# A one-column copy that holds GpSimd's weight remainders back near LayerNorm, two remainders on VectorE, and a new order of the state-space steps

## The chip, the cores and the metric

The kernel runs on one core of a Trainium2 chip. Its time is the device time of one execution in microseconds (us). The engines are named as the profile names them: PE is TensorE's matmul, PEld its weight load, DVE is VectorE, ACT is ScalarE, POOL is GpSimd, SP is SyncE, whose queue issues nearly all loads. L233 is line 233 of the kernel before.

## The reference

One sequence of 512 positions with 1024 channels goes through two residual layers, in float32. Each layer has a token mixer and then a SwiGLU channel mixer of hidden size 2816, and behind each of these four stands a LayerNorm with a residual:

```python
def reference(x, ...):
    h = x
    for i in range(DEPTH):                      # DEPTH = 2
        if i % 2 == 0:
            mix = s5_mixer(h, ...)              # state-space scan over positions, GELU, GLU, out-projection
        else:
            mix = stick_breaking_mixer(h, ...)  # 16 heads x 64, strictly causal, no softmax
        h = layer_norm(DEEPNORM_ALPHA * h + mix, ...)
        h = layer_norm(DEEPNORM_ALPHA * h + swiglu_ffn(h, ...), ...)
    return h
```

## The kernel before

**Split operands.** All large products run on PE in float32r, three matmuls for one (`mm3`, L350 to L352; `tm`, L369 to L371): an operand w is split in a high part (`wh`, a copy on ACT that rounds) and a remainder (`wl` = w - wh). The `Weights` object streams the weight chunks of 128 x 1024 through a ring of 37 buffers of 128 x 1024 (`Ring`, first in, first out). `load` issues the DMA on SP's queue (L226, L223 for pairs), `pump` splits chunk after chunk (L283 on ACT, L286 for the remainder). The remainder is formed on DVE unless `l_eng` names POOL. Activations are split in the same way (`xh`, `xl`; L345 on ACT, L346 on DVE).

**Feed-forward weights in pairs.** From the third row of blocks on (i = 2 to 21) the gate and up weights of a block are combined in seven operands (`split_pair`, through the helper `tt` at L233) for a product with fewer multiplications (`pair`). POOL does three operations of it: half of `s` (128 x 512), the remainder `gl` (128 x 1024) and half of `bl` (128 x 512). DVE does the rest. The x side needs sums and differences of halves of x, formed once per layer by `x_forms` on DVE (L422, then L346 into the tiles `xf`).

**The stages in order.** `ssm` (state space, PE order written out in `SSM_ORDER`), `ssm_end` (GLU and out-projection), `ffn(0)`, `attention`, `att_end` (its out-projection), `ffn(1)`. Where two stages meet, `tail` runs: for each of four tiles of 128 positions the last product steps of the projection, then LayerNorm `ln` on DVE (L390 residual, L392 and L394 statistics, L400 subtract and scale, L80 to L90 the inverse root, L403 the last step), then `tr`, which transposes the tile on PE (L415) and splits it. While the last tile is in LayerNorm, PE already starts the next stage on the first half of the positions (`nxt[0](lo)`, `nxt[1](lo)`). `tail` has `forms=True` behind the two mixers (called by `proj`), False behind the feed-forwards.

**Who remainders go to in `tail`.** From tile t = 1 on, `l_eng` is POOL, until `tail` ends. Inside the product steps of `proj`, `ws.pump(chunks[-1] + 2 * t)` at t = 1 and t = 2 splits the first feed-forward chunks ahead of their use. Behind attention (`begun=7`) only the last of eight chunks is left for t = 0 and 1, so that only t = 2 pumps, four chunks at once; behind the state space one chunk at t = 1 and two at t = 2 are left to pump. When the second half of the positions starts (`run` in `ffn_first`), the first weight pair (chunk i = 2) is split; the pair i = 3 is begun inside `pair(2)`.

**What sets the order.** Inside `tc.manual_schedule(engines=...)` the named engines run in program order: PE, DVE, ACT, POOL and SP in `ssm`; PE and DVE in `pair`. Elsewhere a planner orders each engine's queue by priority and readiness; `high_priority` puts LayerNorm ahead of other DVE work. In `SSM_ORDER` each word is a step with a block number: t, T transpose g on PE (L822), m, M multiply with x (L833), d9 nine filler matmuls (L840), k the kernel matrix (L867) whose result goes through DRAM (L876 out, L889 back in, step n), r and s the scan on DVE, y the output (L957), u a GLU part, p a weight chunk with its remainder on POOL, q one with its remainder on DVE, e a table on POOL.

Of the kernel before, what the change touches and what calls it, by code (L numbers as in the profile page):

```python
# [9 lines left out]
F32 = mybir.dt.float32  # L10
# [7 lines left out]
S = 512  # L18
D = 1024
KD = D // 128  # L20
# [25 lines left out]
def glu_items(text):  # L46
# [12 lines left out]


SSM_ORDER = (
# [3 lines left out]
)  # L65

# [93 lines left out]
class Ring:  # L160


    def __init__(self, pool, n):
        self.pool, self.free, self.n = pool, list(range(n)), 0
        self.slot = {}

    def get(self, name, dtype=F32R):
        i = self.free.pop(0)
        self.n += 1
        t = self.pool.tile([128, 1024], dtype, tag=f"s{i}", bufs=1, name=f"{name}_{self.n}")  # L170
        self.slot[t.name] = i
        return t
# [25 lines left out]
class Weights:  # L198


    def __init__(self, nc, ring):
        self.nc, self.ring = nc, ring
        self.src, self.raw, self.hl = [], {}, {}
        self.loaded = self.split = 0
        self.nraw = 3
        self.hold = True
        self.h_eng = self.l_eng = None

    def add(self, ap):
        self.src.append(ap)  # L210
# [19 lines left out]
    def split_pair(self, i, g, u):  # L230

        nc, V, G_, get = self.nc, self.nc.vector, self.nc.gpsimd, self.ring.get
        tt = lambda o, a, b, op=SUB, e=V: e.tensor_tensor(out=o, in0=a, in1=b, op=op)  # L233
        f = lambda t: t.bitcast(F32)
        lo, hi = slice(0, 512), slice(512, 1024)
        s1, s2 = self.sums
        gh, gl, bh, bl, c, sh, sl = tiles = [get("wf") for _ in range(7)]

        a = [(gh[:, lo], gl[:, lo]), (gh[:, hi], gl[:, hi]), (sh[:, hi], sl[:, hi]), (bh[:, lo], bl[:, lo]),
             (bh[:, hi], bl[:, hi]), (c[:, lo], c[:, hi]), (sh[:, lo], sl[:, lo])]  # L240
        self.hl[i] = dict(tiles=tiles, a=a)
        s = get("ws", F32)
        tt(s[:, lo], g[:, lo], u[:, lo], SUB, G_)
        nc.scalar.activation(gh, g, AF.Copy)  # L244
        nc.scalar.activation(bh[:, lo], u[:, hi], AF.Copy)
        tt(gl, g, f(gh), SUB, G_)
        tt(bl[:, lo], u[:, hi], f(bh[:, lo]), SUB, G_)
        yield
        tt(s1, u[:, lo], u[:, hi], ADD)
        tt(s2, s1, g[:, lo])  # L250
        tt(s[:, hi], g[:, hi], s2)
        nc.scalar.activation(bh[:, hi], s1, AF.Copy)
        nc.scalar.activation(c[:, lo], s2, AF.Copy)
        nc.scalar.activation(sh, s, AF.Copy)
        tt(bl[:, hi], s1, f(bh[:, hi]))
        tt(c[:, hi], s2, f(c[:, lo]))
        yield
        tt(sl, s, f(sh))
        self.ring.put(g, u, s)
        self.split += 1  # L260
        self.load(i + 1)

    def begin(self, i):

# [5 lines left out]
    def pump(self, upto):  # L270
        nc = self.nc
        upto = min(upto, len(self.src) - 1)
        while self.split <= upto:
            i = self.split
            self.load(i if isinstance(self.src[i], tuple) else i + self.nraw - 1)
            w = self.raw.pop(i)
            if isinstance(w, list):
                for _ in self.split_pair(i, *w):
                    pass
                continue  # L280
            h, l = self.ring.get("wh"), self.ring.get("wl")
            if self.h_eng is None:
                nc.scalar.activation(h, w, AF.Copy)  # L283
            else:
                self.h_eng.tensor_copy(h, w)
            (self.l_eng or nc.vector).tensor_tensor(out=l, in0=w, in1=h.bitcast(F32), op=SUB)  # L286
            self.ring.put(w)
            self.load(i + self.nraw)
            self.hl[i] = (h, l)
            self.split += 1  # L290
# [10 lines left out]
class Trunk:  # L301
# [195 lines left out]
    def tail(self, tiles, nxt, out=None, lag=1, fine=False, forms=False):  # L497


        def store(t):  # L500
            if out is None:
                with self.tc.high_priority(offset=1):
                    self.tr(t)
        todo = 0
        for t in range(4):
            steps = tiles[t]
            if t == 1:
                self.ws.l_eng = self.nc.gpsimd
            at = [max(0, len(steps) - 3)] if t >= lag and (t < 3 or not nxt) else []
            if t == 3 and lag > 1:  # L510
                at = [len(steps) // 4, len(steps) // 2]
            for i, f in enumerate(steps):
                if i in at and todo < t:
                    store(todo)
                    todo += 1
                f()
            with self.tc.high_priority(offset=800):
                self.ln(t, self.COLS[t == 3 and fine], None if out is None else out[t])
        self.ring.put(self.lng, self.lnb)
        if nxt:  # L520
            lo, hi = slice(0, S // 2), slice(S // 2, S)
            nxt[0](lo)
            if todo == 2:
                store(2)
            nxt[1](lo)
            if forms:
                E = mybir.EngineType
                f, g = self.x_forms(2), self.x_forms(3)
                next(f)
                next(g)  # L530
                with self.tc.manual_schedule(engines={E.Activation, E.DVE}):
                    next(f)
                    self.tr(3)
                    next(g)
                    for h in (f, g):
                        for _ in h:
                            pass
            else:
                store(3)
            nxt[0](hi)  # L540
            nxt[1](hi)
        else:
            store(3)
        self.ws.l_eng = None

    def ffn(self, l, nxt, out=None):
        nc, ws, ring = self.nc, self.ws, self.ring
# [13 lines left out]
        def ahead():  # L561

            ws.hold = True
            ws.pump(self.c_dn[l][0])
            yield
            take(1)
            yield
            ws.pump(self.c_dn[l][1])
            yield

        for i in range(KF):
            if i > 1:
                c = self.c_gu[l][i]
                if i == 2:
                    self.cv = ring.get("cv", F32)
                E = mybir.EngineType
                with self.tc.manual_schedule(engines={E.PE, E.DVE} | ({E.Activation} if i == KF - 1 else set())):
                    a = ws.get(c, 0)["a"]
                    self.pair(i, a, ws.begin(c + 1) if i < KF - 1 else ahead())
                ws.done(c)  # L580
            else:
                b = 2 * i
                s = self.tmp.tile([128, S], F32, tag="s", name="s")
                nc.scalar.activation(s, self.ps[:, b], AF.Silu)
                nc.vector.tensor_tensor(out=self.hidden(i), in0=s, in1=self.ps[:, b + 1], op=MUL)  # L585
# [500 lines left out]
    def proj(self, chunks, yt, nxt, order=None, begun=0):  # L1086

        ws, ring = self.ws, self.ring
        order = order or list(range(KD))
        tiles = []  # L1090
        for t in range(4):
            steps = []
            todo = [(m, c, n) for m, c in enumerate(self.COLS[t == 3]) for n in range(KD)]
            if t == 0:
                todo.sort(key=lambda a: a[2])
            for m, c, n in todo:
                    k = order[n]
                    if t < 2 and n < begun:
                        continue
                    def f(t=t, n=n, k=k, m=m, c=c):  # L1100
                        hl = ws.get(chunks[k], 0)
                        self.tm(t, hl, yt[k][:, 0:S], yt[k][:, S:], n == 0, n == KD - 1, (c,))
                        if t == 3 and m == 2:
                            ws.done(chunks[k])
                            ring.put(yt[k])
                        if m == 1 and n == 3 and t > 0 and t < 3:
                            ws.pump(chunks[-1] + 2 * t)
                    steps.append(f)
            tiles.append(steps)
        self.tail(tiles, nxt, lag=2 if begun else 1, fine=True, forms=True)  # L1110
# [317 lines left out]
```

## Time and profile before

| | |
|---|---|
| median of 3 runs | 1215.75 us (1214.12 to 1216.79) |
| profiled execution, its own time | 1223.04 us |
| its span, first to last instruction | 1221.3 us |
| mean granted TensorE clock | 0.991 |
| busy: PE, DVE, ACT, POOL | 1164.6, 897.0, 512.1, 383.4 us |
| POOL remainders of pairs (L233) | 80, 161.2 us busy |
| POOL remainders of chunks (L286) | 20, 49.5 us busy |

The profiled execution is one run with the profiler on, and a few microseconds longer than the plain runs. The page gives for each engine the time in which it worked. The list of waits gives, for an engine and line, who ended the wait, the total, how often, and the longest. A timeline row has start, duration, engine, line, operation, output and inputs, shapes, count, and in brackets the idle time of the engine just before with the one who ended it. A windows row has the stretch and the busy time in it of each engine, with the count of instructions that began.

### The profile page before, as it was taken

What the parts mean: (1) busy time and instruction counts of PE and PEld (TensorE: products, weight loads), DVE (VectorE), ACT (ScalarE), POOL (GpSimd) and SP (SyncE); (2) the same over time, 40 slices, a digit from 0 to 9 for tenths busy, and PEclk for the clock granted to TensorE, in tenths of its full rate; (3) what the DMA queues carried; (4) which work ended last, traced back from release to release, by engine and by line L of the source; (5) the groups of instructions that cost most, each with busy time, mean ns of one, the idle gap of its engine ahead of it and who ended that gap; (6) DMA issues with size and microseconds to landing.
All of it is one profiled execution on the core that took longest, in us unless ns stands there. A gap on an engine that the chain in (4) does not pass through costs nothing.

```text
span 1221.3 us, 20799 instructions
## 1 busy us (share of the span) xinstructions
PE 1164.6 (95%) x8494; PEld 1041.3 (85%) x8494; DVE 897.0 (73%) x1403; ACT 512.1 (42%) x813; POOL 383.4 (31%) x320
## 2 busy tenths in 40 slices
PE   3899899999999999999999999998899999999996
PEld 3767688899999999888887888877899999998885
DVE  8898475798788777535867787877977778885436
ACT  1345363044454444431156665652344444444300
POOL 6544402034554551001312222223145555520000
PEclk9999999999999999999999999999899999999999
DMA  5433652023323226432201121230223232254201
GB/s 195 97 96 80 169 190 82 1 87 104 122 70 122 87 102 209 139 104 69 104 15 55 53 70 53 70 104 35 87 92 109 95 109 99 87 202 161 69 18 52
DMA packets 44799, 117.91 MB, mean 97 GB/s; under 512 B 6816, under 2 KB 18080, under 8 KB 44576
## 3 DMA queue, kind: packets, MB, share of 16 engines
q1 hardware_dynamic: 43552, 116.07, 28.8%
q8 instruction: 66, 1.08, 0.4%
q10 hardware_dynamic: 1152, 0.52, 0.3%
q14 instruction: 29, 0.24, 0.1%
HBM read 112.51 MB, written 4.06 MB: 95 GB/s over the span
## 4 chain that ended last, share of the span: by engine, by line
PE 83%; DVE 7%; DMA 2%; ACT 2%; issue 1%; POOL 1%; SPq 0%; DVEq 0%; POOLq 0%; ACTq 0%
PE psum L350 16%; PE psum L352 15%; PE psum L351 15%; PE psum L370 9%; PE psum L371 9%; PE psum L369 9%; PE psum L957 3%; DVE nb L1196 1%; PE psum L1218 1%; PE psum L1283 1%; DVE wl L286 1%; PE psum L1285 1%; PE psum L1284 1%; ACT wh L283 1%; PE psum L415 1%
## 5 line engine op out<-in xcount | busy, mean ns | idle before, releaser
L233 POOL TENSOR_TENSOR wf<-raw,wf 128x1024 fp32r<-128x1024 f32 (+1 forms) x80 | 161.2, 2031 | 217.0 <-ACT wf L244 96.4
L351 PE MATMUL psum<-xf,wf 128*128 128x256 f32 x640 | 181.1, 283 | 0.6 <-DVE wf L233 0.6
L352 PE MATMUL psum<-xf,wf 128*128 128x256 f32 x640 | 181.5, 284 | 0.0
L350 PE MATMUL psum<-xf,wf 128*128 128x256 f32 x640 | 181.2, 283 | 0.0
L286 DVE TENSOR_TENSOR wl<-raw,wh 128x1024 fp32r<-128x1024 f32 x88 | 116.8, 1338 | 64.3 <-ACT wh L283 45.6
L350 PE MATMUL psum<-xh,wh 128*128 128x512 f32 (+1 forms) x416 | 147.8, 356 | 1.8 <-ACT xh L980 1.3
L283 ACT ACTIVATE wh<-raw 128x1024 fp32r<-128x1024 f32 x108 | 112.3, 1053 | 81.4 <-PE psum L371 28.3
L352 PE MATMUL psum<-xl,wh 128*128 128x512 f32 (+1 forms) x416 | 142.3, 345 | 1.3 <-DVE xl L346 0.8
L351 PE MATMUL psum<-xh,wl 128*128 128x512 f32 (+1 forms) x416 | 142.1, 343 | 0.0
L371 PE MATMUL psum<-wh,hid 128*128 128x512 f32 x352 | 137.7, 391 | 0.0
L370 PE MATMUL psum<-wl,hid 128*128 128x512 f32 x352 | 137.4, 390 | 0.0
L369 PE MATMUL psum<-wh,hid 128*128 128x512 f32 x352 | 137.3, 390 | 0.0
L350 PE MATMUL psum<-xh,wf 128*128 128x256 f32 x480 | 134.7, 281 | 0.5 <-DVE hid L585 0.5
L352 PE MATMUL psum<-xl,wf 128*128 128x256 f32 x480 | 133.9, 279 | 0.0
L351 PE MATMUL psum<-xh,wf 128*128 128x256 f32 x480 | 133.9, 279 | 0.0
L286 POOL TENSOR_TENSOR wl<-raw,wh 128x1024 fp32r<-128x1024 f32 x20 | 49.5, 2482 | 253.3 <-DVE wl L286 150.1
L351 PEld LDWEIGHTS psum<-xf,wf 128*128 128x128 f32 x640 | 122.2, 191 | 0.8 <-DVE wf L233 0.8
L350 PEld LDWEIGHTS psum<-xf,wf 128*128 128x128 f32 x640 | 122.6, 192 | 0.0
L352 PEld LDWEIGHTS psum<-xf,wf 128*128 128x128 f32 x640 | 122.2, 191 | 0.0
L350 PEld LDWEIGHTS psum<-xh,wf 128*128 128x128 f32 x480 | 90.4, 188 | 0.7 <-DVE hid L585 0.7
L453 DVE TENSOR_TENSOR cv<-cv,psum 128x512 f32<-128x512 f32 x80 | 54.6, 683 | 49.5 <-PE psum L352 43.3
L350 PEld LDWEIGHTS psum<-xh,wh 128*128 128x128 f32 x416 | 79.4, 191 | 12.7 <-issue 2.8
(222 smaller groups left out, 2700.4 us busy)
## 6 DMA issues: line engine op xcount, KB each, us to landing
raw<-w_gu SPq DMA_DIRECT2D x88, 512.0 KB, 3.5
raw<-w_down SPq DMA_DIRECT2D x44, 512.0 KB, 3.8
raw<-w_glu SPq DMA_DIRECT2D x16, 512.0 KB, 5.0
raw<-w_qk SPq DMA_DIRECT2D x16, 512.0 KB, 3.3
raw<-w_out SPq DMA_DIRECT2D x8, 512.0 KB, 3.5
raw<-w_v SPq DMA_DIRECT2D x8, 512.0 KB, 3.6
raw<-w_o SPq DMA_DIRECT2D x8, 512.0 KB, 3.2
xres<-xs SPq DMA_DIRECT2D x4, 512.0 KB, 6.8
```

What stands on the lines that cost most here:

```text
L233: tt = lambda o, a, b, op=SUB, e=V: e.tensor_tensor(out=o, in0=a, in1=b, op=op)
L283: nc.scalar.activation(h, w, AF.Copy)
L286: (self.l_eng or nc.vector).tensor_tensor(out=l, in0=w, in1=h.bitcast(F32), op=SUB)
L350: mm(out=out, lhsT=sh, rhs=mh, start=first, stop=False)
L351: mm(out=out, lhsT=sl, rhs=mh, start=False, stop=False)
L352: mm(out=out, lhsT=sh, rhs=ml, start=False, stop=last)
L369: mm(out=o, lhsT=sh[:, ts], rhs=hl[0][:, c], start=first, stop=False)
L370: mm(out=o, lhsT=sh[:, ts], rhs=hl[1][:, c], start=False, stop=False)
L371: mm(out=o, lhsT=sl[:, ts], rhs=hl[0][:, c], start=False, stop=last)
L415: nc.tensor.transpose(out=pt[:, k], in_=self.xres[:, t, f:f + 128], identity=self.ident)
L453: tt = lambda o, a, b, op=ADD: V.tensor_tensor(out=o, in0=a, in1=b, op=op)
L957: nc.tensor.matmul(out=yp[rows, j], lhsT=a, rhs=m_, start=step == 0, stop=step == 2)
```

## The change

`Weights` gets a field `after` and a helper `late(t)`: while `after` is set, POOL first copies one column of `after` into the tile that it will write, so that its operation comes behind the writer of `after`. It is used in three places. Behind the two mixers, once the last weight chunk of the projection is met at t = 0, `after` is the last column of that chunk's remainder, for the POOL remainders of `pump`. Once all four LayerNorms are issued, `after` is the last element of x in tile 3, which is LayerNorm's last step; it holds the first weight pair. In `pair(2)` it is the last element of the last x sum's remainder; it holds the second pair (in both feed-forwards). For a pair, three copies are made, one for each tile that POOL writes. Behind the mixers `l_eng` becomes POOL at t = 2 instead of t = 1, and behind attention two chunks are pumped at t = 0, with their remainders on DVE. In `SSM_ORDER` nine fillers move ahead of T0, m0 moves ahead of fillers, and further on a GLU part and a POOL chunk move forward.

```diff
 SSM_ORDER = (
-    "x c0 e0 g0 j0 t0 T0 d9 h0 b0 i0 m0 M0 k0 n0 d9 d9 r0 d9 d9 d9 d9 s0 B0 c1 p e1 y0 g1 t1 j1 T1 z0 m1 M1 h1 l0 "
-    "u1 i1 c2 p u1 k1 n1 p r1 u1 u1 u1 e2 s1 p g2 y1 j2 t2 T2 z1 m2 M2 h2 p i2 c3 k2 n2 u1 e3 r2 l1 p u1 u1 s2 y2 "
+    "x c0 e0 g0 j0 t0 d9 T0 m0 d9 h0 b0 i0 M0 k0 n0 d9 r0 d9 d9 d9 d9 s0 B0 c1 p e1 y0 g1 t1 j1 T1 z0 m1 M1 h1 l0 "
+    "u1 u1 i1 c2 p p k1 n1 p r1 u1 u1 u1 e2 s1 g2 y1 j2 t2 T2 z1 m2 M2 h2 p i2 c3 k2 n2 u1 e3 r2 l1 p u1 u1 s2 y2 "
     "g3 t3 j3 T3 z2 m3 M3 h3 i3 k3 p n3 u1 l2 r3 u1 s3 p q y3 q w0 z3 a w4 l3 q q q"
 )
...
         s = get("ws", F32)
+        for x in (s, gl, bl):
+            self.late(x)
         tt(s[:, lo], g[:, lo], u[:, lo], SUB, G_)
...
+    def late(self, t):
+
+        if self.after is not None:
+            self.nc.gpsimd.tensor_copy(t[:, 0:1], self.after)
...
+            if self.l_eng is not None:
+                self.late(l)
             (self.l_eng or nc.vector).tensor_tensor(out=l, in0=w, in1=h.bitcast(F32), op=SUB)
...
-            if t == 1:
+            if t == (2 if forms else 1):
                 self.ws.l_eng = self.nc.gpsimd
...
         self.ring.put(self.lng, self.lnb)
+        if forms:
+            self.ws.after = self.xres[:, 3, D - 1:D]
         if nxt:
...
-        self.ws.l_eng = None
+        self.ws.l_eng = self.ws.after = None
...
                     a = ws.get(c, 0)["a"]
+                    ws.after = self.xf[3][1][:, 3, S // 2 - 1:S // 2].bitcast(F32) if i == 2 else None
                     self.pair(i, a, ws.begin(c + 1) if i < KF - 1 else ahead())
...
                         hl = ws.get(chunks[k], 0)
+                        if t == 0 and n == KD - 1:
+                            if begun:
+                                ws.pump(chunks[-1] + 2)
+                            ws.after = hl[1][:, D - 1:D].bitcast(F32)
                         self.tm(t, hl, yt[k][:, 0:S], yt[k][:, S:], n == 0, n == KD - 1, (c,))
```

More of the change, by code (lines that the diff above doesn't have):

```diff
@@ L206, in __init__ @@
         self.hold = True
-        self.h_eng = self.l_eng = None
+        self.h_eng = self.l_eng = self.after = None
     def add(self, ap):
```

## The prediction

> **What bounds the kernel now.** I read the page first (engine shares), then whom PE waited for, then the timelines of DVE, POOL and PE in the stretches where PE stands still, then windows for the clock.
>
> ```profile
> PE 1164.6 (95%) x8494; PEld 1041.3 (85%) x8494; DVE 897.0 (73%) x1403; ACT 512.1 (42%) x813; POOL 383.4 (31%) x320
> ```
>
> ```profile
> PE psum L822 <- DVE g L646: 20.2, 2, 18.6
> PE psum L867 <- issue: 5.2, 4, 1.6
> PE psum L415 <- DVE xres L403: 4.6, 1, 4.6
> PE psum L370 <- DVE wl L286: 3.0, 1, 3.0
> ```
>
> TensorE sets the time. It is idle for 1221.3 - 1164.6 = 56.7 us, 18.6 of them at the start, where nothing can run yet. The two longest later waits, 4.6 and 3.0 us, both end at DVE, and both lie where the attention layer ends. At the end of the state-space layer (255 to 300 us, windows summed) PE is idle for 45.00 - 42.88 = 2.1 us, by its list of waits all on DVE but for a last 0.2 on ACT:
>
> ```profile
> sum 45.00, PE 42.88 PEld 42.04 DVE 39.79 ACT 24.56 POOL 22.30; mean PE 0.95 PEld 0.93 DVE 0.88 ACT 0.55 POOL 0.50
> ```
>
> ```profile
> PE psum L350 <- ACT xh L345: 0.2, 1, 0.2
> ```
>
> Why is DVE late? Four rows of the first layer end (DVE's last LN step for an earlier tile and for tile 3, what POOL did meanwhile, and a window: its length, then busy time of PE, weight loads, DVE, ACT and POOL, the granted clock, the DMA share and GB/s), then one of POOL and two of DVE a little later:
>
> ```profile
> 244.89 0.75 DVE L403 SCALAR_TENSOR_TENSOR xres<-xres,rq_y,lnb 128x512 f32<-128x512 f32 x1
> 255.93 3.99 DVE L403 SCALAR_TENSOR_TENSOR xres<-xres,rq_y,lnb 128x512 f32<-128x512 f32 x2
> 256.52 5.68 POOL L233 TENSOR_TENSOR wf<-raw,wf 128x1024 fp32r<-128x1024 f32 x2
> 257.00:260.00 3.00, 3.00 (x28) 3.00 (x28) 2.92 (x2) 0.46 (x2) 3.00 (x2) 1.00 0.01 3
> ```
>
> ```profile
> 271.85 4.12 POOL L233 TENSOR_TENSOR wf<-raw,wf 128x512 fp32r<-128x512 f32 x2 [9.65 <-DVE xf L346]
> ```
>
> ```profile
> 271.69 0.68 DVE L346 TENSOR_TENSOR xf<-psum,xf 128x512 fp32r<-128x512 f32 x1
> ```
>
> ```profile
> 273.62 2.89 DVE L346 TENSOR_TENSOR xf<-u,xf 128x512 fp32r<-128x512 f32 x1
> ```
>
> A step that takes 0.75 alone (1.4 the pair) took 3.99 the pair while POOL formed remainders, with DMA at 0.01, so memory traffic is not the cause. A remainder of x's sums with one input in PSUM kept its 0.68 as POOL began; one with both inputs in SBUF took 2.89. So DVE operations with two SBUF inputs stand still while POOL works on SBUF, for up to a whole POOL operation.
>
> **The change at the attention layer's end, first stall.** Today POOL forms three w_gu remainders beside attention's last steps:
>
> ```profile
> 828.91 7.52 POOL L286 TENSOR_TENSOR wl<-raw,wh 128x1024 fp32r<-128x1024 f32 x3 [14.36 <-ACT wh L283]
> 832.16 2.06 DVE L346 TENSOR_TENSOR oT<-of,oT 128x512 fp32r<-128x512 f32 x1 [1.03 <-ACT oT L345]
> 834.26 3.25 DVE L286 TENSOR_TENSOR wl<-raw,wh 128x1024 fp32r<-128x1024 f32 x1
> 837.57 0.79 PE L370 MATMUL psum<-wl,oT 128*128 128x512 f32 x1 [3.03 <-DVE wl L286]
> 837.50:840.75 3.25, 3.18 (x8) 2.56 (x9) 1.77 (x4) 1.06 (x1) 1.97 (x1) 0.55 0.00 0
> ```
>
> After the change POOL's two remainders here wait for exactly that last weight (by a one-column copy), and two others go to DVE behind it. Undisturbed, the same two kinds take
>
> ```profile
> 793.28 0.69 DVE L346 TENSOR_TENSOR oT<-of,oT 128x512 fp32r<-128x512 f32 x1 [1.22 <-ACT oT L345]
> ```
>
> ```profile
> 794.35 1.22 DVE L286 TENSOR_TENSOR wl<-raw,wh 128x1024 fp32r<-128x1024 f32 x1
> ```
>
> so the last weight's ends at 832.16 + 0.69 + 1.22 = 834.1, before PE wants it at 834.54. The 3.03 goes, and with it the half clock that follows (0.55 over 3.25 us, 1.6 lost): PE is 4.6 earlier. That is no gain by itself, since LN and PE meet again 38 us later.
>
> **Second stall, LN of tile 3.**
>
> ```profile
> 860.00:872.30 12.30, 12.30 (x106) 12.18 (x104) 10.95 (x22) 2.60 (x4) 5.81 (x3) 1.00 0.44 169
> ```
>
> ```profile
> 867.70 2.85 POOL L233 TENSOR_TENSOR wf<-raw,wf 128x1024 fp32r<-128x1024 f32 x1
> 866.57 1.71 DVE L400 SCALAR_TENSOR_TENSOR xres<-xres,mv,lng 128x512 f32<-128x512 f32 x1
> 868.33 2.76 DVE L400 SCALAR_TENSOR_TENSOR xres<-xres,mv,lng 128x512 f32<-128x512 f32 x1
> 876.99 0.47 PE L415 MATMUL psum<-ident,xres 128*128 128x128 f32 x1 [4.61 <-DVE xres L403]
> 876.90:881.80 4.90, 4.81 (x23) 4.58 (x24) 4.13 (x8) 3.38 (x7) 0.00 (x0) 0.54 0.01 3
> ```
>
> POOL's three operations for the first weight pair (5.81 by the window) lie on LN. The two L400 steps (0.75 alone, like L403) cost 1.71 + 2.76 - 1.50 = 3.0 extra. With POOL held until LN's last step, that goes. The rest is DVE's own queue, whose only pauses between the stalls are:
>
> ```profile
> 838.82 0.69 DVE L390 SCALAR_TENSOR_TENSOR xres<-xres,psum 128x512 f32<-128x512 f32 x1 [1.31 <-PE psum L371]
> 853.51 0.69 DVE L390 SCALAR_TENSOR_TENSOR xres<-xres,psum 128x512 f32<-128x512 f32 x1 [0.76 <-PE psum L371]
> 865.17 0.69 DVE L346 TENSOR_TENSOR xl<-psum,xh 128x512 fp32r<-128x512 f32 x1 [1.35 <-ACT xh L345]
> ```
>
> So DVE, not PE, is the bound there, and the two remainders that move to it count in full: 2 x 1.22. They start at 834.1 and collide with POOL's next remainder; the collision costs between 0 and 2 x (3.25 - 1.22) = 4.1; I take 1.0, since the POOL operation that starts at the same moment can hold one of them only in part. LN starts at 834.1 + 2.4 + 1.0 = 837.5 instead of 838.82: 1.3 earlier. The pauses of 0.76 and 1.35 go, since PE (and the loads and ACT work released by it) come 4.6 earlier: 2.1 more, or nothing if other waits replace them. LN of tile 3 then ends 1.3 + 2.1 + 3.0 = 6.4 earlier. PE restarts at 870.6. It arrives at 872.4 - 4.6 = 867.8, so it still waits 2.8, and I leave the half clock behind the wait as it is. **Attention end: -6.4**, bounds -1.2 (LN starts only at 834.1 + 6.5 = 840.6, no pause goes) and -7.8 (rival 1).
>
> What is queued behind the new waits: POOL's three operations for the first weight pair (5.8) and three copies. A one-column copy isn't in the trace; the nearest is the first row here, and the second is PE's first read of that pair:
>
> ```profile
> 14.71 0.19 POOL L734 COPY pk<-pk 128x8 f32<-128x8 f32 x1
> 891.35 0.28 PE L350 MATMUL psum<-xh,wf 128*128 128x256 f32 x1
> ```
>
> I take 0.2 each, 0.6 in all (0.1 to 0.3 each). POOL starts 0.7 after PE's restart and is done 7.1 after it; PE first reads the pair 891.35 - 876.99 = 14.4 after it today, 12.0 without the half clock. Hidden, with 4.9 to spare; gone, it would cost what exceeds that. DVE's own steps for the pair may collide with the delayed POOL work; the same microseconds cover them.
>
> **State-space layer's end.** The L403 pair saves 3.99 - 1.50 = 2.5, the xf remainder 2.89 - 0.68 = 2.2. DVE gains near 5 us, but PE is only idle for 2.1 there, and the 0.2 on ACT stays: **-1.9** (0 to -2.1). The second pair's remainders now wait for x's last sum, which the 4.7 saved bring to near 272; two of POOL's operations start only at 271.85 today, behind a buffer that DVE frees, so this wait delays little. One weight's remainder moves to DVE near 203, where DVE next pauses 7.4:
>
> ```profile
> 215.00 1.37 DVE L390 SCALAR_TENSOR_TENSOR xres<-xres,psum 128x512 f32<-128x512 f32 x2 [7.40 <-PE psum L371]
> ```
>
> so it costs nothing (1.22 were the pause gone).
>
> **The new order at the start.**
>
> ```profile
> 22.15 1.94 PE L822 MATMUL psum<-ident,g 128*128 128x128 f32 x8 [1.59 <-DVE g L646]
> ```
>
> ```profile
> 23.88 4.04 PE L840 MATMUL psum<-ident 128*128 128x128 f32 x18
> 27.86 2.16 PE L833 MATMUL psum<-xres,gt 128*64 128x64 f32 x64
> ```
>
> ```profile
> 33.61 12.32 PE L840 MATMUL psum<-ident 128*128 128x128 f32 x108
> ```
>
> ```profile
> 30.16 1.22 DVE L646 TENSOR_TENSOR w<-e,psum 128x1024 f32<-128x1024 f32 x1 [1.10 <-PE psum L833]
> ```
>
> Nine filler matmuls move into the 1.59 pause, so PE works without a break from 18.6. From start to start, eight transposes take 1.73 and the fillers 3.98 at half speed: the second transposes start at 18.6 + 1.7 + 4.0 = 24.3 instead of 22.15. Full speed (12.32 for 108, half of the 4.04 for 18) comes today some time after 5.7 us of unbroken work, and I take it from 24.3 on: transposes 0.9, half of L833 1.1, the other fillers 2.0, the rest of L833 1.1, end at 29.4 instead of 30.0. **-0.6**, bounds +0.8 (half speed until 27.9 as now) and -0.9 (DVE's last h ends at 30.16 - 1.10 = 29.06). The later moves (a GLU part and one POOL remainder earlier) leave PE's order as it is: 0. They put one load ahead of k1's DMAs in SP's queue (rival 4).
>
> **Sum.** -0.6 - 1.9 - 6.4 = -8.9. The profiled execution took 1223.04 (span 1221.3); it becomes 1214.1. The median of the runs is 7.3 lower, so 1215.75 - 8.9 = 1206.9.
>
> [...]
>
> **Rivals.**
> 1. The clock stays full behind the shorter wait: 2.4 of half clock saved, less the 1.0 that PE then waits for ACT and DVE as at the other layer end: -1.4, 1205.5. Moved idle time could also spare a halving in the state-space layer, 1.6 each: down to 1202.3. Against: the 3.03.
> 2. DVE fills up at the attention end: both moved remainders wait out a POOL operation, LN starts 3 later, the pauses stay: -1.2 there, -3.7 in all, 1212. For: DVE has only 1.31 + 0.76 + 1.35 = 3.4 of pauses in 27 us.
> 3. The change doesn't do what it says: POOL isn't what holds LN, or the collisions only move onto x's sums. Only the start counts: 1215. [...] Against: 3.99 beside 1.41.
> 4. Slower: the load of a weight now stands before k1's two DMAs on SP's queue. If its buffer is not free, everything of block 1 waits:
>
> ```profile
> 73.34 2.15 SPq L876 DMA_DIRECT2D kd<-ksb  x2
> ```
>
> ```profile
> 83.94 1.31 SPq L226 DMA_DIRECT2D raw<-w_glu  x3
> ```
>
> Up to 83.94 - 73.34 = 10.6, plus 1.6 of half clock, against 8.3 gained elsewhere: +3.9, 1219.7. It decides from a block of 7 us. Against: by the ring's order the load takes a buffer of block 0, whose work was over before 45 us.
>
> **How the numbers follow.** Main case 50%, since DVE's queue can be followed row by row (its own range 1204.5 to 1209.5: the collision's 0 to 2, one pause kept or not, the start's bounds), rival 1 15%, rival 2 19%, rival 3 9%, rival 4 7%. A measurement here tells about 0.2% (2.4 us) from no change. Faster: main, rival 1 and nearly all of rival 2: 0.83. Same: rival 3 and a little of rival 2: 0.10. Slower 0.07. The range 1202.5 to 1213 leaves out rivals 3 and 4 and the tails of 1 and 2.
>
> **What the profile after should show.** L403 and L400 of tile 3 at 0.75 in both layer ends; oT remainder 0.7 and the last w_o remainder 1.2, with no PE wait at L370; PE's wait at L415 near 2.8; POOL idle until LN's last step, then copies of about 0.2; nine L840 between the two L822 groups. It would be wrong if L415 still waits over 4 us (DVE's queue), if PE waits for wf from POOL, or if SP's L226 holds L876.

## The result and the profile after

| | before | after |
|---|---|---|
| median, same chip | 1216.27 us (4 runs, 1214.12 to 1217.81) | 1203.54 us (4 runs, 1201.96 to 1205.72) |
| ratio, 95% interval | | 0.9898 (0.9873 to 0.9923) |
| profiled execution, span | 1223.04, 1221.3 us | 1201.96, 1200.2 us |
| mean granted clock | 0.991 | 0.998 |

The change makes the kernel 12.4 us faster (0.0102 of 1216.27); 8.9 were forecast. The two profiled executions are 21.1 apart, because that of before was 6.8 above the median of its runs and that of after 1.6 below (a profiled execution is not always the longer one). So the 21.1 have to be sorted into what the change did and what differs from one execution to the next. Line numbers have moved: L286 is L295, L346 is L355, L370 is L379, L390 is L399, L400 is L409, L403 is L412, L415 is L424, L822 is L834, L840 is L852, L867 is L879; the copies of `late` are L268.

The page's engine row and PE's list of waits, after:

```profile
PE 1156.9 (96%) x8494; PEld 1035.8 (86%) x8494; DVE 894.0 (74%) x1406; ACT 512.5 (43%) x813; POOL 378.6 (32%) x333
```

```profile
PE psum L834 <- DVE g L658: 19.2, 2, 18.8
PE psum L879 <- issue: 2.9, 3, 1.0
PE psum L424 <- DVE xres L412: 0.3, 1, 0.3
```

The wait of 3.0 for the last weight is gone from the list, and the 4.6 for LN's last step is 0.3. Both profiles hold the same 8494 matmuls, so the start of the same matmul in each cuts them into the same stages. Stage ends: the projection's first matmul, the first use of the first weight pair, the first matmul on attention's last split output (832.18 before, 821.84 after), the first use of the pair in the second feed-forward (891.35 and 870.27), the last matmul.

| stage, us | before | after | difference |
|---|---|---|---|
| state space, from the first matmul | 185.93 | 176.87 | -9.06 |
| end of the state space, to the pair | 71.74 | 70.30 | -1.44 |
| feed-forward and attention | 555.89 | 555.88 | 0 |
| end of attention, to the pair | 59.18 | 48.43 | -10.75 |
| rest | 319.73 | 319.73 | 0 |

**The end of attention.** DVE, POOL and PE in time order, after:

```profile
818.04 2.36 DVE L295 TENSOR_TENSOR wl<-raw,wh 128x1024 fp32r<-128x1024 f32 x2 [0.46 <-ACT wh L290]
821.82 0.69 DVE L355 TENSOR_TENSOR oT<-of,oT 128x512 fp32r<-128x512 f32 x1 [0.69 <-ACT oT L354]
822.55 1.23 DVE L295 TENSOR_TENSOR wl<-raw,wh 128x1024 fp32r<-128x1024 f32 x1
824.68 1.28 DVE L399 SCALAR_TENSOR_TENSOR xres<-xres,psum 128x512 f32<-128x512 f32 x2 [0.90 <-PE psum L380]
850.09 0.74 DVE L409 SCALAR_TENSOR_TENSOR xres<-xres,mv,lng 128x512 f32<-128x512 f32 x1
850.87 0.74 DVE L409 SCALAR_TENSOR_TENSOR xres<-xres,mv,lng 128x512 f32<-128x512 f32 x1
856.72 1.41 DVE L412 SCALAR_TENSOR_TENSOR xres<-xres,rq_y,lnb 128x512 f32<-128x512 f32 x2
```

```profile
823.84 0.30 POOL L268 CAST wl<-wl 128x1 fp32r<-128x1 f32 x2 [20.09 <-DVE wl L295]
824.10 4.78 POOL L295 TENSOR_TENSOR wl<-raw,wh 128x1024 fp32r<-128x1024 f32 x2
858.26 0.18 POOL L268 COPY ws<-xres 128x1 f32<-128x1 f32 x1 [29.38 <-PE psum L424]
858.38 0.30 POOL L268 CAST wf<-xres 128x1 fp32r<-128x1 f32 x2
```

```profile
821.84 1.19 PE L378 MATMUL psum<-wh,oT 128*128 128x512 f32 x4 [0.41 <-ACT oT L354]
857.52 1.32 PE L424 MATMUL psum<-ident,xres 128*128 128x128 f32 x8 [0.27 <-DVE xres L412]
870.27 0.28 PE L359 MATMUL psum<-xh,wf 128*128 128x256 f32 x1
```

The DVE steps that the prediction named are back at their size: oT's remainder 0.69 (it was 2.06), the last weight's 1.23 (3.25), the two steps of tile 3 0.74 (1.71 and 2.76). POOL waits 29.38 us and starts behind LN's last step with one copy of 0.18 and two that take 0.30 together. The first row is the one the prediction had wrong: the two moved remainders stand at 818.04, in a pause ahead of attention's last step.

**The end of the state space**, after:

```profile
247.06 1.42 DVE L412 SCALAR_TENSOR_TENSOR xres<-xres,rq_y,lnb 128x512 f32<-128x512 f32 x2
260.48 1.29 DVE L355 TENSOR_TENSOR xf<-u,xf 128x512 fp32r<-128x512 f32 x2
262.88 3.51 DVE L355 TENSOR_TENSOR xf<-u,xf 128x512 fp32r<-128x512 f32 x2
```

```profile
262.67 2.57 POOL L233 TENSOR_TENSOR wf<-raw,wf 128x1024 fp32r<-128x1024 f32 x1 [8.78 <-ACT wf L246]
```

LN's last pair is at 1.42 again (3.99 before). One pair of remainders of x's sums still takes 3.51 where the pair before it took 1.29, because POOL forms a pair's remainder beside it (262.67). No one-column copy stands ahead of that remainder, so it belongs to a pair that no wait holds: the planner put a later pair ahead of the one that the third wait holds.

**The start.** PE after, then PE and SP's queue before, then SP's queue after:

```profile
18.80 1.94 PE L834 MATMUL psum<-ident,g 128*128 128x128 f32 x8 [18.80 <-DVE g L658]
20.53 4.05 PE L852 MATMUL psum<-ident 128*128 128x128 f32 x18
24.37 1.17 PE L834 MATMUL psum<-ident,g 128*128 128x128 f32 x8
29.84 0.32 PE L879 MATMUL psum<-cc,g 64*32 64x16 f32 x16
```

```profile
29.94 0.32 PE L867 MATMUL psum<-cc,g 64*32 64x16 f32 x16
32.92 0.27 PE L867 MATMUL psum<-cc,g 64*32 64x16 f32 x10 [0.99 <-issue]
34.14 1.72 SPq L876 DMA_DIRECT2D kd<-ksb  x2
36.81 5.42 SPq L889 DMA_DIRECT2D xl<-kd  x8
```

```profile
32.84 0.89 SPq L888 DMA_DIRECT2D kd<-ksb  x2
34.78 5.44 SPq L901 DMA_DIRECT2D xl<-kd  x8
69.06 1.78 SPq L888 DMA_DIRECT2D kd<-ksb  x2
```

The nine fillers (18 passes) lie between the transposes. The first kernel matrix starts only 0.1 earlier (29.84 against 29.94), but the wait of 0.99 for issue inside it is gone, and the transfer that feeds the first output is issued 2.0 earlier. The weight load that now stands ahead of the next block's transfers did not hold them up: SP issues them at 69.06 (73.34 before).

### The profile page after: what moved, and what is told of

Same layout as the page of the kernel before. It is cut to its first block, busy times and chain, and to the rows that moved or that the text cites. A ratio compares the mean times of both kernels' runs of the same rounds, so it can differ in the third digit from the quotient of the medians.

```text
span 1200.2 us, 20813 instructions
## 1 busy us (share of the span) xinstructions
PE 1156.9 (96%) x8494; PEld 1035.8 (86%) x8494; DVE 894.0 (74%) x1406; ACT 512.5 (43%) x813; POOL 378.6 (32%) x333
## 4 chain that ended last, share of the span: by engine, by line
PE 83%; DVE 10%; ACT 2%; issue 2%; POOL 2%; DMA 1%; SPq 0%; DVEq 0%; POOLq 0%; ACTq 0%
PE psum L359 16%; PE psum L361 16%; PE psum L360 16%; PE psum L378 8%; PE psum L380 8%; PE psum L379 8%; PE psum L969 2%; DVE nb L1212 1%; PE psum L1234 1%; ACT wh L290 1%; DVE wl L295 1%; PE psum L1299 1%; PE psum L1250 1%; POOL be L1213 1%; PE psum L1249 1%
## 5 line engine op out<-in xcount | busy, mean ns | idle before, releaser
L295 DVE TENSOR_TENSOR wl<-raw,wh 128x1024 fp32r<-128x1024 f32 x91 | 119.6, 1325 | 59.1 <-ACT wh L290 40.3
L290 ACT ACTIVATE wh<-raw 128x1024 fp32r<-128x1024 f32 x108 | 112.4, 1054 | 76.1 <-PE psum L380 25.9
L379 PE MATMUL psum<-wl,hid 128*128 128x512 f32 x352 | 137.5, 391 | 0.0
L295 POOL TENSOR_TENSOR wl<-raw,wh 128x1024 fp32r<-128x1024 f32 x17 | 41.9, 2476 | 177.0 <-DVE wl L295 96.6
L361 PEld LDWEIGHTS psum<-xl,wf 128*128 128x128 f32 x480 | 90.3, 188 | 0.0
```

Of the source, the lines that this page charges most:

```text
L361: mm(out=out, lhsT=sh, rhs=ml, start=False, stop=last)
L379: mm(out=o, lhsT=sh[:, ts], rhs=hl[1][:, c], start=False, stop=False)
```

## The experiments

Each ratio is to runs of the kernel before on the same chip. The last two columns are stages of its profiled execution, as in the table above.

| kernel | median us | ratio, 95% interval | state space | end of attention |
|---|---|---|---|---|
| b_again (before) | 1216.05 | 0.9991 (0.9975 to 1.0008) | 182.12 | 58.49 |
| b_order | 1215.68 | 0.9980 (0.9962 to 0.9998) | 177.61 | 58.66 |
| a_oldorder | 1205.10 | 0.9896 (0.9877 to 0.9914) | 180.02 | 48.43 |
| a_nowait | 1212.54 | 0.9958 (0.9944 to 0.9972) | 178.59 | 52.77 |
| a_lnwait | 1206.92 | 0.9910 (0.9888 to 0.9932) | 180.33 | 49.22 |
| a_noln | 1211.55 | 0.9952 (0.9936 to 0.9968) | 180.39 | 53.68 |
| a_poolrem | 1209.68 | 0.9934 (0.9913 to 0.9955) | 179.19 | 52.63 |
| a_noxf | 1206.69 | 0.9899 (0.9885 to 0.9914) | 180.88 | 48.41 |
| a_again (after) | 1206.18 | 0.9897 (0.9883 to 0.9910) | 180.92 | 48.42 |
| a_fill | 1202.81 | 0.9880 (0.9866 to 0.9893) | 176.49 | 48.42 |
| b_fill | 1218.23 | 0.9998 (0.9983 to 1.0013) | 179.55 | 59.43 |
| b_fill10 | 1217.95 | 0.9999 (0.9982 to 1.0016) | 184.56 | 56.23 |

**b_again: before, unchanged.**

> The kernel before, unchanged, for a second profile and the clocks of its plain runs. In the first profile the clock was halved in five periods of 3.41 us, each behind a period of the same fixed grid in which PE was busy for less than half (0.27 to 0.48; 0.53 and more kept it full). Theory: the grid runs free of the kernel, so which stalls halve the clock differs from run to run; then the two state-space halvings (at 62.2 and 140.7, 1.5 us each) are missing or elsewhere in this profile, and the clock of single runs varies between 0.991 and 0.996. Rival: the program fixes them; then they stand at the same two places again and every run has 0.991. Time by both: 1216.3, 1214 to 1219.

Measured: a span of 1217.5, 3.8 shorter than the first profile, and by stage the 3.8 lie in the state space (185.93 and 182.12). The halving at 62 is there again, the one at 140 is not, so neither text holds in full; single runs have clocks of 0.989 to 0.995 and times of 1213.52 to 1223.56. So the state-space stage of one profile can't be set against that of another to less than about 4 us, while the end of attention repeats within 0.7 (58.49, 58.66, 59.18).

**b_order: the new order alone.**

```diff
-    "x c0 e0 g0 j0 t0 T0 d9 h0 b0 i0 m0 M0 k0 n0 d9 d9 r0 ...
+    "x c0 e0 g0 j0 t0 d9 T0 m0 d9 h0 b0 i0 M0 k0 n0 d9 r0 ...
...
```

> The kernel before with the new state-space order alone. The prediction gave the order -0.6 us (1215.7). Between the two profiles PE gained 8.9 us up to the end of the state space: 2.7 by the first output, 1.5 + 1.5 by two halvings of the clock that are gone, 1.6 by a shorter wait for the last block's kernel matrix, the rest by shorter waits for issue. Theory A: all 8.9 come from the order: 1207.4. Theory B: only the 2.7 at the start come from it, the rest is a difference between single runs: 1213.6. Theory C, as predicted: 1215.7.

Measured: -2.4 by the ratio, -0.2 to -4.6 by its interval. That excludes theory A; B and C both lie inside, so the run can't tell them apart. From the first matmul to the first output the five profiles with the old order take 26.1 to 27.9 (mean 27.1), the nine with the new one 23.6 to 25.9 (mean 24.7).

**a_oldorder: waits and remainders alone.**

```diff
-    (the new SSM_ORDER)
+    (the old SSM_ORDER)
```

> The kernel after with the old state-space order: waits and moved remainders alone. Between the profiles these gave 1.8 us at the end of the state space and 10.4 at the end of attention (the prediction: 1.9 and 6.4). If all of that holds in plain runs: 1216.3 - 12.2 = 1204.1, and the order gives next to nothing. If the prediction's sizes hold: 1208.0. By theory B of the order (2.7): 1203.5 + 2.7 = 1206.2. In its profile PE waits under 1 us for LN's last step behind attention, and not at all for the last weight.

Measured: 0.9896, as much as the whole change. So the two layer ends carry the result: 1.44 and 10.1 to 10.8 by stage, 12.7 by the ratio (10.5 to 15.0).

**a_nowait: no copies.**

```diff
     def late(self, t):
-        if self.after is not None:
-            self.nc.gpsimd.tensor_copy(t[:, 0:1], self.after)
+        return
```

> The kernel after without the one-column copies: order and moved remainders kept, POOL free to work beside LN. Theory: the waits carry the second stall of attention's end (two LN steps held by 3.0 us, PE late by up to 4.6 and 1.6 of half clock behind it) and the 1.8 at the end of the state space, while the moved remainders alone do away with the first stall; then 1203.5 + 3 to 7 = 1206.5 to 1210.5, with L409 of tile 3 over 1.5 us again. Rival: moving the remainders off POOL was enough, the copies do nothing: 1203.5. Second rival: without the waits the first stall stays too: 1213 to 1215.

Measured: 0.9958; by the ratios 7.3 slower than after (0.0060 of 1217.9), just beyond the theory's 3 to 7 (its time, 1206.5 to 1210.5, was missed by 2.0). So the moved remainders alone are not enough. They shorten the end of attention from 58.8 (mean of before, b_again and b_order) to 52.77. The first stall does not go, as the theory had it, but shrinks from 3.0 to 1.0, and oT's remainder is still held. DVE's rows and PE's waits:

```profile
825.38 2.03 DVE L354 TENSOR_TENSOR oT<-of,oT 128x512 fp32r<-128x512 f32 x1 [0.69 <-ACT oT L353]
855.48 1.66 DVE L408 SCALAR_TENSOR_TENSOR xres<-xres,mv,lng 128x512 f32<-128x512 f32 x1
```

```profile
PE psum L423 <- DVE xres L411: 2.5, 1, 2.5
PE psum L378 <- DVE wl L294: 1.0, 1, 1.0
```

**a_lnwait and a_noln: one wait, and the other two.** The first keeps only the wait for LN's last step, the second only the other two.

```diff
-                            ws.after = hl[1][:, D - 1:D].bitcast(F32)
...
-                    ws.after = self.xf[3][1][:, 3, S // 2 - 1:S // 2].bitcast(F32) if i == 2 else None
+                    ws.after = None
```

> The kernel after with only one of the three waits: the first weight pair behind LN's last step. Without any wait the kernel took 1212.5 us, with all three 1203.5. Theory: of these 9, the second stall of attention's end and the half clock behind it (some 4 to 5) and LN of tile 3 at the first layer end (1) belong to this wait; the last weight's wait carries about 1 to 3 (oT's remainder took 2.03 instead of 0.69 without waits, PE stood 1.0 for the last weight), x's sums about 1. So 1206.5 to 1208. Rival: the last weight's wait carries most of it, since a late start of LN carries through to its end: 1210 to 1212.

```diff
-        if forms:
-            self.ws.after = self.xres[:, 3, D - 1:D]
+        self.ws.after = None
```

> The kernel after with the other two waits: last weight and x's sums, but the first weight pair free to be formed beside LN of tile 3. Theory: oT and the last weight's remainder at 0.69 and 1.23, PE not stopped there, L400's counterpart L409 of tile 3 over 1.5 us in one or two steps, PE waits 1 to 3 us for LN's last step: 1206.5 to 1209. Rival (LN was only late because it started late): 1204.

Measured: a_lnwait's 1206.92 is as its theory said, but the unchanged kernel after took 1206.18 on that chip (a_again below). LN's wait alone brings the end of attention to 49.22, 0.8 from all three; PE then waits 0.9 for the last weight. The other two without it leave 53.68, no better than no wait at all (52.77): LN starts 1.2 earlier than there and then meets POOL in full. a_noln's 1211.55 lies above its theory's 1206.5 to 1209. PE waits 3.4 for LN's last step and the clock is half for two periods behind it; and the end of the state space, which the theory left out, takes 74.12 against 70.30. DVE and POOL of a_noln:

```profile
856.13 1.83 DVE L409 SCALAR_TENSOR_TENSOR xres<-xres,mv,lng 128x512 f32<-128x512 f32 x1
858.00 2.77 DVE L409 SCALAR_TENSOR_TENSOR xres<-xres,mv,lng 128x512 f32<-128x512 f32 x1
```

```profile
856.10 1.30 POOL L233 TENSOR_TENSOR ws<-raw,raw 128x512 f32<-128x512 f32 x1 [0.68 <-DMA raw<-w_gu]
857.37 2.85 POOL L233 TENSOR_TENSOR wf<-raw,wf 128x1024 fp32r<-128x1024 f32 x1
```

The two steps together are 3.1 longer than in the profile after, and from LN's first step to tile 3's transposes a_noln takes 35.91 against 32.84, also 3.1 longer. So what POOL holds up here, LN pays in full.

**a_poolrem: the remainders back on POOL, all waits kept.**

```diff
-            if t == (2 if forms else 1):
+            if t == 1:
...
-                            if begun:
-                                ws.pump(chunks[-1] + 2)
```

> The kernel after with the two moved remainders back on POOL (and the one at the first layer end), all waits kept. The prediction counted the two on DVE in full, 3.4 us with a collision; the profile after has them at 818.04 in a pause of DVE ahead of attention's last step, so they cost nothing there. Theory: back on POOL they stand behind the last weight and put 2 x 2.4 us more of POOL beside LN of tiles 0 and 1, which holds two to four LN steps for 1 to 2 us each, and DVE is the bound there: 1205 to 1209. Rival: the place of the remainders does not matter once they wait: 1203.5. Second rival, by the prediction's own term (DVE is 2.4 to 3.4 us freer): 1201.

Measured: 0.9934; by the ratios 4.4 slower than after, inside the theory's 1.5 to 5.5 (as a time, 1209.7 is 0.7 beyond it). Both rivals fall. LN starts as early as after, but four remainders now stand behind the last weight and beside LN of the first tiles; the end of attention takes 52.63.

```profile
826.16 7.57 POOL L295 TENSOR_TENSOR wl<-raw,wh 128x1024 fp32r<-128x1024 f32 x3
```

```profile
832.12 2.16 DVE L409 SCALAR_TENSOR_TENSOR xres<-xres,mv,lng 128x512 f32<-128x512 f32 x1
835.77 1.58 DVE L409 SCALAR_TENSOR_TENSOR xres<-xres,mv,lng 128x512 f32<-128x512 f32 x1
```

**a_noxf: without the third wait.**

```diff
-                    ws.after = self.xf[3][1][:, 3, S // 2 - 1:S // 2].bitcast(F32) if i == 2 else None
+                    ws.after = None
```

> The kernel after without the third wait (second weight pair behind x's last sum), the other two kept. The first wait's kernel (LN alone) took 1206.9, all three 1203.5. Theory: the second pair's remainders then stand beside x's sums and hold two or three of them for 1 to 2 us at both layer ends, but PE has other work there: 1203.5 to 1205. Rival: this wait carries most of the 3.4 us: 1206 to 1207.

Measured: 0.9899 against 0.9897 of a_again on the same chip, and both layer ends within 0.02 (70.29 and 48.41 against 70.30 and 48.42). Behind attention the remainders of x's sums stay at 0.68: the pair's POOL work starts behind them even without the wait. The theory's collisions behind attention do not occur, and the third wait makes no difference to either layer end.

**b_fill and b_fill10: before, with fillers in PE's waits.** No wait is meant to become shorter; only the clock is to change.

```diff
-    ... s3 p q y3 ...
+    ... s3 p q d9 y3 ...        (b_fill alone)
...
-                    self.tr(3)
+                    [self.nc.tensor.matmul(out=self.ps[:, 6, 0:128], lhsT=self.ident, rhs=self.ident, start=True, stop=True) for _ in range(24 * (lag > 1))]; self.tr(3)
```

In b_fill10 the 24 is 10; `lag > 1` holds behind attention alone.

> The kernel before with filler matmuls in two of PE's waits: nine (18 passes, 2.05 us) ahead of the last block's output, where PE waits 1.9 to 3.0 us for a transfer, and 24 (2.7 us) ahead of tile 3's transposes behind attention, where it waits 2.6 to 4.6 us for LN. No wait is shortened. Theory: the clock is halved for 3.41 us whenever PE was busy for less than half of the period before; with fillers these two halvings are gone and only the one behind the last weight's wait (and in some runs one near 62 us) is left: 1.6 to 2.4 us behind attention and 1.5 in those runs that had one at 140 us, so 1214.0 to 1215.5 against 1217.5. Rival (the clock falls for another reason, such as work of other engines): the half clock stays and the time is 1217.5.

> The kernel before with ten filler matmuls ahead of tile 3's transposes behind attention (20 passes, 2.3 us by the 0.114 of a pass; the 24 of the first trial ran for 5.52 and outlasted the wait). The wait for LN stays at 2.6 to 4.6 us, the half clock behind it goes: 1.5 to 2.4 us, 1215.3 to 1216 against 1217.5. Rival (half the clock costs nothing there, since PE then waits for DVE and ACT, as the next engines in the chain): 1217 to 1217.5, with PE waits for ACT and DVE at the first sums in place of the slow matmuls.

Measured: no change in time by either, so both theories' times were missed. In b_fill the two halvings that were aimed at are gone from the profile, but its 24 fillers ran for 5.52, twice what I had reckoned (48 passes, not 24), outlasted the wait, and ate what they saved. In b_fill10 they fit:

```profile
871.20 2.39 PE L533 MATMUL psum<-ident 128*128 128x128 f32 x20
874.53 1.32 PE L415 MATMUL psum<-ident,xres 128*128 128x128 f32 x8 [0.93 <-DVE xres L403]
```

From tile 3's transposes to the pair PE takes 12.75 there, as after (12.75), against 14.36 before and 14.29 in b_again: the half clock behind the stall is worth 1.6, with nothing handed back to other waits. That the median doesn't show it (its interval reaches down to -2.2 us) is not explained; this profile has a longer halving elsewhere, two periods from 136.5.

**a_again and a_fill: after, and after with five fillers in two waits of the state space.**

```diff
-    "u1 u1 i1 c2 ...    ... s3 p q y3 ...
+    "d5 u1 u1 i1 c2 ... ... s3 p q d5 y3 ...
```

> The kernel after, unchanged, beside the other three of this call: 1203.5 (1202 to 1206). By the theory of the clock its runs differ by whether the wait ahead of the last block's output leaves PE busy for less than half of a period: about half of the runs 1.5 to 3 us longer, and none with a halving behind attention.

> The kernel after with five filler matmuls (10 passes, 1.1 us) in each of two waits of PE in the state space: ahead of the first GLU part (1.3 us for ACT) and ahead of the last block's output (1.4 to 2.4 us for a transfer, of which 0.7 is ACT reading the fillers' bank). Theory: neither period falls below half any more, so the slower half of the runs disappears: 1202.0, all runs within 1 us. Rival: the halvings do not decide the spread, the transfer does: 1203.5 with the same spread. If the fillers overshoot their waits: 1204 to 1205.

Measured: 1206.18, a little above what was expected, and 1202.81, on one chip. a_again's profile is halved once, at 60.2; its state space takes 180.92 against 176.87. Three of a_fill's four runs lie at 1202.29 to 1202.87 with clocks of 0.997 and 0.998, the fourth at 1205.95 with 0.995, so the slower runs are not gone, as the theory had it. It is the fastest kernel of this study by its median; its interval and a_again's overlap.

## Why the prediction was right, and where it was wrong

The direction, the place and the mechanism hold: at both layer ends DVE waits for POOL, and what the copies hold back is what had stretched DVE. The time, 1203.5, lies in the range near its low end, because the largest term was too small. It lies below the main case's own 1204.5 to 1209.5: what kept it inside was the room left for rival 1, whose reason is not what happened. That much was luck.

- **End of attention, -6.4: measured -10.75 between the profiles** (-10.1 against b_again), outside the term's own bounds of -1.2 to -7.8. Three parts made the sum. The collisions and pauses, 3.0 + 2.1: from LN's first step to tile 3's transposes 38.17 became 32.84, 5.3 less; right, the steps by 3.0 and the pauses by 2.3. The size of the collision is not the same in every execution, though: in b_again the same two steps took 0.73 and 1.66, and the stretch 37.65 all the same; what took up the difference is open. LN's start, 1.3: behind the last split output it came at 6.64 (838.82 - 832.18, next fence) and now at 2.84 (824.68 - 821.84), 3.8 earlier. This step failed: I counted the two moved remainders in full behind the last weight (2.4 + 1.0), but they run at 818.04 in DVE's pause before it, and LN waits 0.90 for PE. I had looked for pauses between the two stalls and not ahead of the first, where the trace of before has them (same fence: 2.42 and 2.02). The half clock, 0: I kept it, with a wait of 2.8 left. The wait is 0.3, so it went, 1.6. The two mis-sized parts are 2.5 and 1.6 of the missing 4.3.

```profile
827.73 0.68 DVE L1240 TENSOR_TENSOR of<-of,psum 64x512 f32<-64x512 f32 x1 [2.42 <-ACT of L1239]
830.43 0.69 DVE L1240 TENSOR_TENSOR of<-of,psum 64x512 f32<-64x512 f32 x1 [2.02 <-ACT of L1239]
832.18 1.20 PE L369 MATMUL psum<-wh,oT 128*128 128x512 f32 x4 [0.15 <-ACT oT L345]
```

- **First stall.** As forecast: last weight's remainder 1.23, no wait of PE for it, no half clock at 837.
- **End of the state space, -1.9: measured -1.44.** LN's pair went to 1.42 as expected; a pair of remainders of x's sums did not (3.51), since another pair's POOL work took that place.
- **Start, -0.6.** The speed did as assumed: the second transposes took 1.17, the first 1.94, near the 1.97 that eight took at a granted clock of 0.54 (before, 876.99). But the first kernel matrix started at 29.84, not 29.4, a gain of 0.1 (inside the bounds), and I stopped the sum there. A wait for issue of 0.40 to 0.99 inside that matrix stands in all five profiles with the old order and in none of the nine with the new one (why PE waits there no trace shows), and the first output comes 2.4 earlier by the means above. How much of that the kernel keeps stays open: 2.4 by b_order, nothing by a_oldorder against the whole change. The sum of the ends, 12.2, already explains 12.4.
- **Hidden work.** POOL's delayed pair held PE nowhere. The copies cost 0.2 each, but for two of 1.2 in the second pairs (270.29 and 873.03) and one of 1.1 at 196.63, where DVE was at work beside them.
- **Rivals.** Rival 1's case came about at the place it named, for another reason (a wait of 0.3, not a kind clock). Rival 2 did not occur: the moved remainders took 2.36 together, undisturbed, and LN started earlier, not later. Rival 3 falls with a_noln, where the steps are held again, and with 0.74 for L409. Rival 4 did not occur.
- **The sum's base.** Taking the profiled execution's 7.3 above the median as given, and not as part of any term, was right: of the profiles' 9.06 in the state space the plain runs keep 2.4 by b_order's ratio, and at most 4.6 by its interval.

Neither half of the change does it alone: moved remainders without waits leave 52.77, waits without moved remainders 52.63, both 48.4, from 58.8. Each takes away POOL work that the other leaves beside DVE's steps.

## What to carry to other kernels

When work is taken off a busy engine, look for the pauses it can fall into ahead of the stall as well as behind it, and follow the queue to the next meeting of the engines before a term is closed. An engine that is a third busy (POOL, 32% after) held a busier one (DVE, 74%) where both read SBUF: a step of 0.74 took 2.77 in a_noln. A one-column copy, 0.18 at 858.26, tied its work to a later step (whether a priority could do the same was not tried). Cut two traces at the same instructions and profile the old kernel twice before explaining a difference: here one stage varied by 4 us with nothing changed, and another by 0.7.

## What the runs showed of the hardware

**In these runs the granted clock was 0.50 for periods of 3.41 us, behind periods in which PE was busy for half or less.** Each fence has two neighbouring periods: length, PE's busy time, granted clock, DMA share, GB/s. b_fill10, then before:

```profile
57.98:61.39 3.41, 1.65 (x34) 1.00 0.00 0
61.39:64.81 3.42, 3.40 (x8) 0.50 0.00 0
```

```profile
96.32:99.73 3.41, 1.82 (x96) 1.00 0.02 5
99.73:103.14 3.41, 3.41 (x18) 1.00 0.22 64
```

Behind 1.65 of 3.41 (0.48) the clock was 0.50, behind 1.82 (0.53) it stayed at 1.00. In before the periods at 0.50 that begin at 62.18, 140.69, 837.01 and 874.55 came behind 1.62, 1.19, 0.93 and 1.24 of 3.41 (0.48, 0.35, 0.27 and 0.36); the last of them, with 0.97 (0.28), was followed by another at 0.50. In each of the fourteen profiles the changes of the granted clock lie whole periods apart (before: half at 62.18, 140.69 and 837.01, 23 and 204 periods from one to the next). Counted over all fourteen up to the last matmul, all 26 periods at full clock with a busy share up to 0.503 were followed by a half one; of those from 0.513 on, two were, both at 0.572 in the attention layer, where the same share also passed without it (a_oldorder). The period in which the last matmul ends does not always follow this: in a_lnwait one of 0.46 was followed by full clock. In a half period 128x512 matmuls started every 0.43 us (before, 838.16 to 839.86) instead of 0.23 (from 840.59), so it costs up to 3.41 x (1 - 0.23 / 0.43) = 1.6 us. By these shares, an estimate: a wait of 2.8 would most often have halved the clock, and one of 1.4 alone, which leaves 0.59 of a period, would not.

**Two DVE steps that began beside a running POOL operation, both with their inputs in SBUF, ended 0.55 us behind it.** In a_noln DVE's step began at 858.00, 0.6 behind the start of a POOL operation of 2.85 that ended at 860.22, and ended 0.55 after it: 2.77 in all, against 0.74 without POOL. In before the second step of LN's last pair began at 257.04, 0.5 behind the start of a POOL operation of 2.86 (256.52), and ended 0.55 after it: 2.88, against 0.75 without POOL.
